# A second wide group in a feed-forward layer, transposes from raw copies, and three weight sums made earlier, in a two-layer hybrid trunk

## The chip, the cores and the metric

The kernel runs on one core of a Trainium2 chip. The metric is the device time of one execution in microseconds (us). Before the change the median of three runs is 2246.27 us (2244.93 to 2246.49).

## The reference, cut to what matters

Two layers over a sequence of 256 tokens of width 2048, batch 1, all in fp32. The mixers (a state-space scan beside block attention in layer 0, sparse attention beside retention in layer 1) are left out here; the change touches what stands around them.

```python
def layer_norm(x, g, b):
    mu = x.mean(-1, keepdims=True); var = jnp.square(x - mu).mean(-1, keepdims=True)
    return (x - mu) * lax.rsqrt(var + 1e-5) * g + b
# each layer, ALPHA = 4 ** 0.25:
#   x = layer_norm(ALPHA * x + mixer(x))
#   x = layer_norm(ALPHA * x + ffn(x))
# ffn: a and u are x @ w_up (2048 -> 5632 each), a depthwise causal convolution of 3 taps along the
#   tokens and a SiLU on a, then (a * u) @ w_down (5632 -> 2048)
```

## The kernel before, in words

**Numbers and products.** An fp32 value is split into a high part in fp32r (a 32-bit type that TensorE multiplies in one pass) and a low rest, and a product is the sum of high x high, high x low and low x high. Activations stand transposed in tiles `x` and `g`: 128 channels (a "k-tile") on the partitions, and along the free axis 256 tokens of high parts and 256 of low parts. Weights come as slabs of 128x1024 (two k-tiles of 512 columns, 512 KB): SP's queue loads `wraw`, ScalarE makes `whi` (L211), VectorE makes `wlo` (L219).

**Groups.** A projection is a row of groups, and PE runs them one behind the other. `group_b` (L432) makes 256 output channels from 16 k-tiles, in two halves of 128: for each k-tile and half a matmul of 512 columns with `whi` and one of 256 with `wlo`, so 64 matmuls for 2048 input channels. `group_m` (L544 to L546, "wide") makes the 1024 channels of four such groups, and takes two k-tiles (a pair) at a time with seven block products in place of eight (Strassen's way). It needs sums of weight blocks. A pair of k-tiles is plain ("P"), or its sums are made while it runs, by four VectorE adds in `add_up` (L230, "N"), or it reads sums that were made earlier and stored ("R", a "kept set"). A kept set is made by `Weights.make`: POOL's queue loads 1 MB of weights into `sums` (L241), VectorE adds (L251), POOL's queue stores the sums to `sumdown` (L255). `cycles` spaces these three steps over a list.

**The feed-forward layer** (`ffn`) has 44 groups of the up projection, for channel block j an a-group and a u-group. Where j is in `WIDE_UP`, one `group_m` of 180 matmuls takes the place of four groups (a and u of j and of j+1). Before, layer 0 has one (j = 7) and layer 1 has three (4, 8, 12). Such a result comes out with tokens on the partitions. It is put together in the tile `other` by VectorE adds (L562) and must be transposed on TensorE by sixteen 128x128 transposes in four bursts (`turn`, L1712). In layer 1 these are fp32 transposes straight from `other` with the matrix `ident`. In layer 0 each quarter of `other` is first copied by a DMA of POOL's queue into the fp32r tile `turned` (L1665), and the transposes run in fp32r with `unit`, a copy of the identity in that type. The tiles of a wide group (`other`, `turned`, `room`) lie in a pool that is given back after group `FIRST`.

**The norms.** The mixers and the first feed-forward layer leave their output in `r` (tokens on the partitions). There are three norms inside the trunk (idx 0, 1, 2) and one at its end. Their first k-tiles are normalized ahead (`norm`); `norm_full` does the others in pairs, while the first group of the next projection runs: four transposes of `r` (L847, fp32 with `ident`), then ScalarE and VectorE scale and split into `x`. When it has transposed k-tiles 4 and 5, it subtracts the mean and scales on VectorE for k-tiles 8 to 11 (`centre`, L798, one instruction for each token half), and with k-tiles 8 and 9 the same for 12 to 15. The group of L432 that runs meanwhile needs k-tile after k-tile of `x`.

**Order.** Steps that belong beside a projection lie in two lists, `self.fill` and `self.aux`; one step of each is taken between k-tiles. A scheduler then sets the order of each engine; instructions under `pin` keep the order of the program among themselves.

Of the kernel before, what the change touches and what calls it, by code (L numbers as in the profile page):

```python
# [9 lines left out]
F32 = mybir.dt.float32  # L10
F32R = mybir.dt.float32r
# [24 lines left out]
WIDE_UP = ((7,), (4, 8, 12))  # L36
FIRST = (22, 30)
# [16 lines left out]
EARLY = 2  # L54
# [272 lines left out]
class Trunk:  # L327
# [194 lines left out]
    def group_m(self, act, src, p, c, gap=1, fresh=None, inner=None):  # L522
# [26 lines left out]
        def fold():  # L549
# [3 lines left out]
            if fresh is not None or inner:  # L553
# [16 lines left out]
                for q, z in zip((0, 2, 1, 3), ((0, 0, "P2", e, OP.add), (1, 0, "P4", h, OP.subtract),  # L570
                                               (0, 1, "P3", g, OP.add), (1, 1, "B8", i, OP.add))):
                    fill.add(lambda z=z, q=q: (last(*z), self.copy and inner and self.copy(q)))
                if inner:
                    inner([[e, g], [h, i]])
# [265 lines left out]
    def norm_full(self, idx, k0):  # L840
# [4 lines left out]
        for i, k in enumerate(ks):  # L845
            for t in range(2):
                nc.tensor.transpose(ps[:, 256 * i + 128 * t:256 * i + 128 * t + 128], r[:, t, 128 * k:128 * k + 128],  # L847
                                    self.ident)
# [317 lines left out]
    def even(self):  # L1166
        nc, x = self.nc, self.x
        with ExitStack() as ctx:
# [63 lines left out]
            with self.tc.tile_pool(name="even2", bufs=1) as P2:  # L1232
# [8 lines left out]

                for i in range(4):
# [10 lines left out]
                    self.pair(heads, (2, 1, 1) if i < 2 else (0, 1, 1))  # L1253
                self.fill.rate = 1.0
# [153 lines left out]
    def odd(self):  # L1408
        nc, x = self.nc, self.x
        with ExitStack() as ctx:  # L1410
            P = ctx.enter_context(self.tc.tile_pool(name="odd", bufs=1))
            self.zbufs = 4
            y = P.tile([128, KT, 512], F32R, name="y")
            with self.tc.tile_pool(name="odd2", bufs=1) as P2:
# [85 lines left out]
                early = self.keys("down1")[:EARLY]  # L1500
                self.cycles(early, [slots], 14, self.aux)
# [134 lines left out]
    def ffn(self, layer):  # L1636
        nc, x = self.nc, self.x
        with ExitStack() as ctx:
# [9 lines left out]
            keys = self.keys("down0", "od_out") if layer == 0 else self.keys("down1")[EARLY:]  # L1648
            left = [double]
            if wide:  # L1650
                E = early.enter_context(self.tc.tile_pool(name="early", bufs=1))
                other = self.w.other = E.tile([128, 2048], F32, name="other")
                room = E.tile([128, 1024], F32, name="room")
# [7 lines left out]
            self.copy = None  # L1661
            if layer == 0:
                turned, unit = E.tile([128, 4, 512], F32R, name="turned"), E.tile([128, 128], F32R, name="unit")
                nc.scalar.activation(unit, self.ident, AF.Copy)
                self.copy = lambda q: self.pin(nc.gpsimd.dma_start(turned[:, q, :].bitcast(F32),  # L1665
                                                                   other[:, 512 * q:512 * q + 512]))
# [38 lines left out]
            def inner(j0):  # L1705
                def turn(j, own, evac):
# [176 lines left out]
```

## Time and profile before

| what | number |
|---|---|
| median of three runs | 2246.27 us (2244.93 to 2246.49) |
| the profiled execution's own time | 2247.41 us |
| its span in the profile | 2245.6 us |
| granted TensorE clock, mean | 0.999 |
| layer 0's feed-forward up projection and what follows up to the next mixer | about 378 to 861 us |
| layer 1's | from about 1527 us |

Rows that begin with an engine are one instruction, or a run of alike ones: start in us, length in us, engine, line of the kernel, operation, output<-inputs (buffer numbers left out), tile sizes, count, and in brackets how long the engine was idle ahead of it and what ended that. "128*128" is the weight block of a matmul. A matmul's length reaches over its pipeline, so two in a row overlap and the pitch between starts is the cost. Rows of windows give for each engine its busy time and its count of instructions in a stretch, the granted clock ("PEclk", 1.00 is full), the share of DMA time and GB/s. In a row of DMA issues the last number is the median time in us from the issue to the landing of the data.

### The profile page before, as it was taken

To read this page: it belongs to the slowest core of one execution; us is meant where nothing else is said; L and a number is where in the kernel's file an instruction comes from. 1 tells how busy PE (TensorE), PEld (TensorE's weight loads), DVE (VectorE), ACT (ScalarE), POOL (GpSimd) and SP (SyncE) were. 2 spreads that over 40 slices of the span, in tenths; PEclk is the share of its full clock that TensorE was granted. 3 is DMA by queue.
4 is the path that set the end of the run, shared out by engine and by line. 5 is a ranking of instruction groups with operands and counts; after the bars stand their busy time and mean duration, and the time that the engine had idled before them with its cause. 6 is when DMAs were issued, how large, how long until landed. Compare 5 with 4: busy or idle time off the path is not lost.

```text
span 2245.6 us, 32854 instructions
## 1 busy us (share of the span) xinstructions
PE 2236.6 (100%) x12061; PEld 1920.2 (86%) x12061; DVE 1829.0 (81%) x2772; ACT 1253.6 (56%) x1719; POOL 128.9 (6%) x223
## 2 busy tenths in 40 slices
PE   9999999999999999999999999999999999999998
PEld 9888888888888888888898888888888888888887
DVE  5788688988877778887977877889998887779887
ACT  5555556655655556656545564457555565557563
POOL 0101000110111110000000000000100001100000
PEclk9999999999999999999999999999999999999999
DMA  8855456796888886888667644567866768878784
GB/s 312 292 174 161 158 195 185 274 376 215 276 307 307 306 301 217 293 282 278 208 216 275 225 157 154 147 209 235 274 224 215 245 215 273 300 268 275 274 283 167
DMA packets 159098, 547.36 MB, mean 244 GB/s; under 512 B 17891, under 2 KB 19347, under 8 KB 158803
## 3 DMA queue, kind: packets, MB, share of 16 engines
q1 hardware_dynamic: 132937, 451.41, 60.4%
q0 software_dynamic: 25856, 93.60, 11.7%
q8 instruction: 94, 1.54, 0.3%
q14 instruction: 67, 0.55, 0.1%
q10 hardware_dynamic: 144, 0.26, 0.0%
HBM read 502.19 MB, written 41.96 MB: 242 GB/s over the span
## 4 chain that ended last, share of the span: by engine, by line
PE 96%; DVE 2%; issue 1%; DMA 1%; ACT 0%; POOL 0%; SPq 0%; ACTq 0%; DVEq 0%; POOLq 0%
PE acc L432 51%; PE ps L545 7%; PE ps L544 7%; PE ps L546 7%; PE acc L632 3%; PE acc L545 3%; PE acc L633 3%; PE acc L546 3%; PE acc L634 3%; PE acc L544 3%; PE ps L634 1%; PE ps L633 1%; PE ps L632 1%; PE ps L1160 1%; PE ps L432 1%
## 5 line engine op out<-in xcount | busy, mean ns | idle before, releaser
L211 ACT ACTIVATE whi<-wraw 128x1024 fp32r<-128x1024 f32 (+4 forms) x882 | 875.0, 1002 | 544.6 <-PE acc L432 215.1
L219 DVE TENSOR_TENSOR wlo<-wraw,whi 128x1024 fp32r<-128x1024 f32 (+4 forms) x882 | 1006.7, 1152 | 201.1 <-ACT whi L211 189.5
L432 PE MATMUL acc<-x,whi 128*128 128x512 f32 x3296 | 1033.1, 399 | 0.0
L432 PEld LDWEIGHTS acc<-x,wlo 128*128 128x128 f32 x3296 | 604.5, 188 | 135.8 <-DVE wlo L219 0.3
L432 PE MATMUL acc<-x,wlo 128*128 128x256 f32 x3296 | 634.4, 279 | 0.0
L432 PEld LDWEIGHTS acc<-x,whi 128*128 128x128 f32 x3296 | 511.0, 189 | 10.1 <-issue 0.9
L694 ACT ACTIVATE tmp<-acc 128x512 f32<-128x512 f32 x104 | 62.2, 598 | 169.2 <-PE acc L432 169.1
L251 DVE TENSOR_TENSOR sums<-sums 128x512 f32<-128x512 f32 (+1 forms) x112 | 87.5, 781 | 21.1 <-DMA sums<-in_down 19.5
L544 PE MATMUL ps<-whi,g 128*128 128x512 f32 x260 | 101.3, 390 | 0.1
L545 PE MATMUL ps<-wlo,g 128*128 128x512 f32 x260 | 101.4, 390 | 0.0
L546 PE MATMUL ps<-whi,g 128*128 128x512 f32 x260 | 101.3, 390 | 0.0
L545 PE MATMUL ps<-wlo,x 128*128 128x512 f32 x244 | 95.7, 392 | 0.1
L546 PE MATMUL ps<-whi,x 128*128 128x512 f32 x244 | 95.1, 390 | 0.0
L544 PE MATMUL ps<-whi,x 128*128 128x512 f32 x244 | 94.5, 390 | 0.0
L632 PE MATMUL acc<-whi,x 128*128 128x344 f32 (+3 forms) x224 | 75.3, 339 | 0.1
L633 PE MATMUL acc<-wlo,x 128*128 128x344 f32 (+3 forms) x224 | 74.7, 333 | 0.0
L1690 DVE SCALAR_TENSOR_TENSOR c<-fpad,prm,c 128x256 f32<-128x256 f32 x176 | 74.0, 479 | 0.8 <-ACT c L1687 0.7
L634 PE MATMUL acc<-whi,x 128*128 128x344 f32 (+3 forms) x224 | 74.4, 332 | 0.0
L211 ACT ACTIVATE whi<-other 128x1024 fp32r<-128x1024 f32 x32 | 33.7, 1054 | 54.9 <-DVE other L230 54.5
L255 POOL DMA_DIRECT2D sumdown<-sums x58 | 31.2, 537 | 527.0 <-DVE sums L251 526.7
L544 PEld LDWEIGHTS ps<-whi,g 128*128 128x128 f32 x260 | 48.8, 188 | 10.7 <-DVE r L712 0.5
L545 PEld LDWEIGHTS ps<-wlo,g 128*128 128x128 f32 x260 | 48.8, 188 | 10.5 <-DVE wlo L219 0.4
(465 smaller groups left out, 3144.5 us busy)
## 6 DMA issues: line engine op xcount, KB each, us to landing
wraw<-in_up SPq DMA_DIRECT2D x328, 512.0 KB, 4.8
wraw<-in_down SPq DMA_DIRECT2D x142, 512.0 KB, 4.9
wraw<-in_od_in SPq DMA_DIRECT2D x96, 512.0 KB, 4.1
wraw<-in_ev_in SPq DMA_DIRECT2D x72, 512.0 KB, 4.1
wraw<-sumdown SPq DMA_DIRECT2D x68, 512.0 KB, 4.9
sums<-in_down POOLq DMA_DIRECT2D x58, 512.0 KB, 7.1
sumdown<-sums POOLq DMA_DIRECT2D x58, 512.0 KB, 4.9
wraw<-in_ev_out SPq DMA_DIRECT2D x30, 512.0 KB, 3.9
```

What stands on the lines that cost most here:

```text
L211: a = nc.scalar.activation(hi[:, :n], raw[:, :n], AF.Copy)
L219: b = nc.vector.tensor_tensor(lo[:, :n], raw[:, :n], hi[:, :n].bitcast(F32), op=OP.subtract)
L251: self.tc.keep_in_program_order(nc.vector.tensor_tensor(o, x, y, op=OP.add))
L432: nc.tensor.matmul(acc, wt, mv, start=(k == 0 and i < len(unit)), stop=(k == nk - 1 and i >= len(unit)))
L544: nc.tensor.matmul(o, xh, wh, start=n not in used, stop=False)
L545: nc.tensor.matmul(o, xh, wl, start=False, stop=False)
L546: nc.tensor.matmul(o, xl, wh, start=False, stop=stop)
L632: nc.tensor.matmul(o, xh, wh, start=start, stop=False)
L633: nc.tensor.matmul(o, xh, wl, start=False, stop=False)
L634: nc.tensor.matmul(o, xl, wh, start=False, stop=stop)
L694: nc.scalar.activation(t, a[:, :, 256:], AF.Copy, scale=sign)
L1690: nc.vector.scalar_tensor_tensor(c[:, i, :], pad[:, i, t:t + 256], w[:, t:t + 1], c[:, i, :], op0=OP.mult, op1=OP.add)
```

## The change

- Layer 0's wide groups are 4 and 8 in place of 7, and `FIRST` for layer 0 is 24 in place of 22.
- In layer 1 the wide groups 4 and 8 (not 12, the last) are turned from raw copies too: after the group's last L562, one DMA of 128x4x256 (512 KB, POOL's queue) brings the columns of block j, a second one those of j+1, and the transposes run in fp32r with `unit`. `turned` takes the room of `room`, which is given back when the first wide group starts.
- In the norms 0, 1 and 2, right after each `centre` of k-tiles 8 to 11 and 12 to 15 a DMA on POOL's queue copies the centred 128x512 (256 KB) of `r` into a tile that is free at that time (`part` in the feed-forward layers, `y` in the odd mixer), and `norm_full` transposes these eight k-tiles from the copies, in fp32r.
- `unit` is made once, behind the first mixer, in the tile of `ones`.
- Three kept sets of layer 0's down projection are made during layer 0's attention (list `aux`, one each 14 steps), no longer in its feed-forward layer. Layer 1's two early sets stay.

```diff
-WIDE_UP = ((7,), (4, 8, 12))
-FIRST = (22, 30)
+WIDE_UP = ((4, 8), (4, 8, 12))
+FIRST = (24, 30)
-EARLY = 2
+EARLY = (3, 2)
 # norm_full
-                nc.tensor.transpose(ps[:, 256 * i + 128 * t:256 * i + 128 * t + 128], r[:, t, 128 * k:128 * k + 128],
-                                    self.ident)
+                to, src, by = ps, r[:, t, 128 * k:128 * k + 128], self.ident
+                if k >= 8:
+                    c = 512 * t + 128 * (k % 4)
+                    to, src, by = ps.bitcast(F32R), self.copies[k // 4 - 2][:, c:c + 128], self.unit
+                nc.tensor.transpose(to[:, 256 * i + 128 * t:256 * i + 128 * t + 128], src, by)
...
         if k0 % 4 == 0 and k0 + 4 < KT:
             for t in range(2):
-                self.pin(self.centre(t, 128 * k0 + 512, 512))
+                c = 128 * k0 + 512
+                self.pin(self.centre(t, c, 512))
+                self.pin(nc.gpsimd.dma_start(self.copies[k0 // 4 - 1][:, 512 * t:512 * t + 512].bitcast(F32),
+                                             r[:, t, c:c + 512]))
 # even, ahead of the attention's heads
+                self.aux.add(12)
+                self.cycles(self.keys("down0")[:EARLY[0]], [self.w.sums], 14, self.aux)
 # ffn
-            keys = self.keys("down0", "od_out") if layer == 0 else self.keys("down1")[EARLY:]
+            keys = self.keys(*(("down0", "od_out"), ("down1",))[layer])[EARLY[layer]:]
+                self.copies = self.slots[:1:-1]
 # ffn, inner
+                width = 0 if layer and j0 == wide[-1] else turned.shape[2]
+                def copy(q, c):
+                    src = blocks[:, q, :] if width == 512 else blocks[:, :, c:c + width]
+                    to = turned[:, q, :] if width == 512 else turned
+                    self.pin(nc.gpsimd.dma_start(to.bitcast(F32), src))
...
+                    for i, j in enumerate((j0, j0 + 1)):
+                        if width == 256:
+                            aux.add(lambda i=i: copy(0, 256 * i), 3)
 # warm_up and run
+        self.unit = self.consts.tile([128, 128], F32R, name="ones")
+        nc.scalar.activation(self.unit, self.ident, AF.Copy)
```

How the order of PE moves at the norm ahead of layer 0's feed-forward layer (idx 0), k-tiles 6 and 7 of its first group, with the transposes of k-tiles 8 and 9 among them. Before:

```order
L432 MATMUL acc<-x,whi 128x512 x4
L432 MATMUL ps<-x,whi 128x512 x2
L847 MATMUL ps<-ident,r 128x128 x2
L432 MATMUL acc<-x,wlo 128x256 x4
L432 MATMUL ps<-x,wlo 128x256 x2
L847 MATMUL ps<-ident,r 128x128 x2
L432 MATMUL acc<-x,whi 128x512 x2
L432 MATMUL acc<-x,wlo 128x256 x2
```

After (`part_3662` is the raw copy of k-tiles 8 to 11):

```order
L432 MATMUL acc<-x,whi 128x512 x4
L432 MATMUL ps<-x,whi 128x512 x2
L432 MATMUL acc<-x,wlo 128x256 x4
L432 MATMUL ps<-x,wlo 128x256 x2
L851 MATMUL ps<-ones,part_3662 128x128
L432 MATMUL acc<-x,whi 128x512 x2
L851 MATMUL ps<-ones,part_3662 128x128 x3
L432 MATMUL acc<-x,wlo 128x256 x2
```

Of the four transposes, the first of token half 0 now stands behind six `wlo` matmuls, and the three others two 512-column matmuls later; whatever comes behind them on PE waits until the copies have landed.

How POOL moves in the same place, from the end of layer 0's scan to the start of its feed-forward layer. Before:

```order
L1367 TENSOR_TENSOR xs<-xs 128x256 x3
L1377 TENSOR_TENSOR rms<-rms,mhalf 128x2
L1367 TENSOR_TENSOR xs<-xs 128x256 x3
L1377 TENSOR_TENSOR rms<-rms,mhalf 128x2
L794 TENSOR_TENSOR rs<-mv,mhalf 128x1 x2
L874 DMA room<-in_lnrow 128x512 x2
L241 DMA sums<-in_down 128x1024 x2
L241 DMA second<-in_down 128x1024 x2
```

After, the end of the same stretch (`sumdown_5` is the third of the kept sets that are now made in the attention):

```order
L241 DMA sums<-in_down 128x1024 x2
L255 DMA sumdown_5_0_1764<-sums 128x1024
L255 DMA sumdown_5_1_1765<-sums 128x1024
L794 TENSOR_TENSOR rs<-mv,mhalf 128x1 x2
L866 DMA part_3662<-r 128x512 x2
L866 DMA part_3661<-r 128x512 x2
L880 DMA room<-in_lnrow 128x512 x2
L241 DMA sums<-in_down 128x1024 x2
L241 DMA second<-in_down 128x1024 x2
```

The loads and stores of three kept sets stand ahead of the norm, and the four copies of the norm stand ahead of the loads of the residual's rows (`room`) and of the next kept sets.

More of the change, by code (lines that the diff above doesn't have):

```diff
@@ L571, in fold @@
                                                (0, 1, "P3", g, OP.add), (1, 1, "B8", i, OP.add))):
-                    fill.add(lambda z=z, q=q: (last(*z), self.copy and inner and self.copy(q)))
-                if inner:
-                    inner([[e, g], [h, i]])
+                    fill.add(lambda z=z: last(*z))
+                    if inner:
+                        inner(q)
                 return
@@ L1660, in ffn @@
                 self.residual(2 * layer, [[self.spare[:, 0:512], self.spare[:, 512:1024]]] * 4)
[L1661 to L1666, printed above, removed]
             if double:
@@ L1705, in inner @@
             def inner(j0):
-                def turn(j, own, evac):
+                turned, aux = turning[0], self.aux
+                width = 0 if layer and j0 == wide[-1] else turned.shape[2]
+                sides = turned if width else other.rearrange("p (q c) -> p q c", q=4)
+                blocks = other.rearrange("p (q c) -> p q c", q=4)
+                def copy(q, c):
+                    src = blocks[:, q, :] if width == 512 else blocks[:, :, c:c + width]
+                    to = turned[:, q, :] if width == 512 else turned
+                    self.pin(nc.gpsimd.dma_start(to.bitcast(F32), src))
@@ L1707, in turn @@
+                def turn(j, n, evac):
                     ps = self.ps()
-                    to, unit_ = (ps.bitcast(F32R), unit) if self.copy else (ps, self.ident)
+                    to, by = (ps.bitcast(F32R), self.unit) if width else (ps, self.ident)
                     for o in range(2):
                         for t in range(2):
-                            c = 256 * (j - j0) + 128 * o
-                            nc.tensor.transpose(to[:, 256 * o + 128 * t:256 * o + 128 * t + 128], own[t][:, c:c + 128], unit_)
+                            c = (256 * (j - j0) + 128 * o) % (width or 512)
+                            nc.tensor.transpose(to[:, 256 * o + 128 * t:256 * o + 128 * t + 128],
+                                                sides[:, 2 * t + n, c:c + 128], by)
@@ L1713, in turn, with go @@
                     evac(ps.rearrange("p (a b) -> p a b", a=2), False)
-                def go(z):
-                    if self.copy:
-                        z = [[turned[:, 2 * t + n, :] for n in range(2)] for t in range(2)]
-                        self.aux.add(3)
-                    for j in (j0, j0 + 1):
+                def go(q):
+                    if width == 512:
+                        aux.q.append(lambda last=aux.q.pop(): (last(), copy(q, 0)))
+                    if q < 3:
+                        return
+                    for i, j in enumerate((j0, j0 + 1)):
+                        if width == 256:
+                            aux.add(lambda i=i: copy(0, 256 * i), 3)
+                        elif width and i == 0:
+                            aux.add(2)
@@ L1720, in go @@
                         for n, f in enumerate((ev_a, ev_u)):
-                            self.aux.add(1, lambda j=j, n=n, f=f: turn(j, [z[t][n] for t in range(2)], f(j)))
+                            aux.add(1, lambda j=j, n=n, f=f: turn(j, n, f(j)))
                 return go
@@ L1735, in ffn @@
                     assert not self.aux.q
+                    if j == wide[0]:
+                        rooms.close()
+                        turning.append(rooms.enter_context(self.tc.tile_pool(name="turned", bufs=1)).tile(
+                            [128, 4, 256 if layer else 512], F32R, name="turned"))
                     self.group_m(x, f"up{layer}", wide.index(j), 0, inner=inner(j))
```

13 lines of the change are left out of this document (8 added, 5 removed).

## The prediction

> **What bounds the kernel now.** I read the page's busy times first, then its chain of waits. The first says which engine has no slack, the second whether that engine also sets the end.
>
> ```profile
> PE 2236.6 (100%) x12061; PEld 1920.2 (86%) x12061; DVE 1829.0 (81%) x2772; ACT 1253.6 (56%) x1719; POOL 128.9 (6%) x223
> ```
>
> The chain, as shares by engine:
>
> ```profile
> PE 96%; DVE 2%; issue 1%; DMA 1%; ACT 0%; POOL 0%; SPq 0%; ACTq 0%; DVEq 0%; POOLq 0%
> ```
>
> PE is busy throughout and carries 96% of the chain, so what PE no longer executes comes off the time, and every wait put into PE's order is added in full. An added copy or sum costs something only where PE comes to wait for it. Windows then give the price of the groups, and how full VectorE (DVE) is where the change loads it.
>
> ```profile
> core 0: us, PE busy (x) PEld busy (x) DVE busy (x) ACT busy (x) POOL busy (x), PEclk, DMA share, GB/s
> 528.38:569.66 41.28, 41.27 (x181) 33.64 (x180) 36.76 (x43) 24.11 (x27) 0.56 (x1) 1.00 0.64 198
> 569.66:861.40 291.74, 291.74 (x1682) 255.10 (x1681) 217.85 (x264) 154.28 (x190) 31.84 (x59) 1.00 0.84 294
> 1610.19:1652.28 42.09, 41.65 (x181) 33.55 (x180) 38.41 (x46) 24.21 (x27) 0.00 (x0) 1.00 0.66 218
> 180.00:276.00 96.00, 96.00 (x607) 84.03 (x606) 68.67 (x134) 50.87 (x89) 8.19 (x7) 1.00 0.50 160
> 378.00:423.00 45.00, 45.00 (x266) 39.42 (x266) 44.60 (x84) 35.01 (x57) 2.13 (x4) 1.00 0.80 272
> 1250.00:1340.00 90.00, 90.00 (x540) 79.83 (x539) 67.29 (x199) 53.44 (x141) 3.75 (x7) 1.00 0.56 188
> ```
>
> The rows are, in this order: layer 0's wide group; the stretch behind it, up to the end of its feed-forward up projection; layer 1's first wide group; layer 0's attention; the start of layer 0's feed-forward layer; layer 1's second half of the mixer. The granted clock is 1.00 everywhere, so it does not enter.
>
> **Cheaper transposes.** A burst of four in fp32r, then one in fp32, each with what stands behind it:
>
> ```profile
> 582.22 0.46 PE L1712 MATMUL ps<-unit,turned 128*128 128x128 f32 x4
> 582.51 0.70 PE L432 MATMUL acc<-x,whi 128*128 128x512 f32 x2
> 583.05 0.28 PE L432 MATMUL acc<-x,wlo 128*128 128x256 f32 x1
> ```
>
> and
>
> ```profile
> 1660.63 0.60 PE L1712 MATMUL ps<-ident,other 128*128 128x128 f32 x4
> 1660.99 0.71 PE L432 MATMUL acc<-x,whi 128*128 128x512 f32 x2
> 1661.54 0.40 PE L432 MATMUL acc<-x,wlo 128*128 128x256 f32 x2
> ```
>
> From start to start: 0.29 + 0.54 = 0.83 against 0.36 + 0.55 = 0.91, so a burst saves 0.08. Two groups of layer 1 have 8 bursts (**-0.6**), three norms with k-tiles 8 to 15 have 12 (**-0.9**). The Trainium skill (FP8 and Floating Point Precision, TensorE Precision Notes) says that true fp32 takes four passes through the array. By that rule an fp32 burst would cost 4 x 0.29 = 1.2 and the 20 bursts would save some 17 us; the rows show 0.36, so the trace does not agree for transposes.
>
> **One more wide group.** The stretch of 291.74 us holds 26 groups of L432 (1664 of its 1682 matmuls), the four bursts of turns and nothing else of size on PE. By the rows above a burst of four fp32r turns costs about 0.37: 0.29, and 0.08 because the two matmuls behind it take 0.54 and not the usual 0.47 or so. So four groups cost (291.74 - 4 x 0.37) / 26 x 4 = 44.7. The wide group that replaces them costs 41.3 and its own four bursts 1.5: a gain of 1.9. Layer 0's first wide group now stands at j = 4, where layer 1's first one stands. That one took 42.1, and its PE waited for `wlo`:
>
> ```profile
> 1614.43 0.51 PE L545 MATMUL acc<-wlo,part 128*128 128x512 f32 x1 [0.44 <-DVE wlo L219]
> ```
>
> DVE's order is the same at that place, so I charge 0.8 for it. Net: **-1.1** (-1.9 without that charge).
>
> **Do the norms' copies come in time?** This is the large term. The rows that set it are those of idx 0: `centre` on DVE, PE at the burst for k-tiles 8 and 9 and at the one for 12 and 13, and, for the time that such a copy takes, layer 0's turns, which copy the same 256 KB from tile to tile on the same queue.
>
> ```profile
> 379.27 1.00 DVE L798 TENSOR_SCALAR r<-r,mv,rs 128x512 f32<-128x512 f32 x2
> 386.64 1.00 DVE L798 TENSOR_SCALAR r<-r,mv,rs 128x512 f32<-128x512 f32 x2
> 381.88 0.38 PE L847 MATMUL ps<-ident,r 128*128 128x128 f32 x2
> 382.19 0.74 PE L432 MATMUL acc<-x,wlo 128*128 128x256 f32 x4
> 383.00 0.38 PE L847 MATMUL ps<-ident,r 128*128 128x128 f32 x2
> 392.06 0.60 PE L847 MATMUL ps<-ident,r 128*128 128x128 f32 x4
> ```
>
> and the turns, with the landing of their copies in the last row:
>
> ```profile
> 574.64 0.68 DVE L562 TENSOR_TENSOR other<-ps,other 128x512 f32<-128x512 f32 x1
> 573.13 0.56 POOL L1665 DMA_DIRECT2D turned<-other  x1 [3.51 <-DVE other L562]
> 574.00 0.55 POOL L1665 DMA_DIRECT2D turned<-other  x1 [0.31 <-issue]
> 575.64 0.55 POOL L1665 DMA_DIRECT2D turned<-other  x1 [1.09 <-DVE other L562]
> L1665 POOL DMA_DIRECT2D turned<-other x4: 546/551/556, 569.1 to 575.6; - x4
> DMA to landing us min/median/max: 4.1/4.6/5.3
> ```
>
> A copy starts 0.3 us behind the DVE instruction that it reads (575.64 against 574.64 + 0.68), and a second one 0.87 behind the first (574.00 - 573.13). The first of the pair's two instructions ends half-way, at 379.8, so the copies start at 380.1 and 381.0, and the second lands at 381.0 + 4.6 = 385.6. By its new order PE is past the six `wlo` matmuls at 382.7 (383.00 less the 0.31 of the two transposes that left), then does one transpose of half 0 and two matmuls (0.5), and needs half 1 at 383.2. First wait: 385.6 - 383.2 = 2.4.
>
> The wait delays the next `centre`, which needs what this burst brings: 3.64 us lie between 383.00 and 386.64. Counted from the burst, its first half ends at 3.64 + 0.5, the copies start at 4.5 and 5.35, and the second lands at 9.95. PE's next burst came 392.06 - 383.00 = 9.06 behind, less the two matmuls that now stand ahead and the burst's own saving: 8.5. Second wait: 1.45. It may be a little shorter. What DVE does with the burst waits for ScalarE's copy of it and for four slabs of `wlo`:
>
> ```profile
> 383.88 0.56 ACT L855 ACTIVATE sums<-ps,prm 128x256 f32<-128x256 f32 x1
> 381.18 3.56 DVE L219 TENSOR_TENSOR wlo<-wraw,whi 128x768 fp32r<-128x768 f32 x4
> 384.65 0.42 DVE L858 TENSOR_TENSOR x<-sums,x 128x256 fp32r<-128x256 f32 x1
> ```
>
> ScalarE ended at 384.44, DVE began at 384.65. While PE stands DVE does these slabs, so I take off that 0.2 and have 1.2, and 3.6 for the norm.
>
> ```profile
> 1098.56 1.00 DVE L798 TENSOR_SCALAR r<-r,mv,rs 128x512 f32<-128x512 f32 x2
> 1528.11 1.00 DVE L798 TENSOR_SCALAR r<-r,mv,rs 128x512 f32<-128x512 f32 x2
> 1105.88 0.60 PE L847 MATMUL ps<-ident,r 128*128 128x128 f32 x4
> 1531.84 0.38 PE L847 MATMUL ps<-ident,r 128*128 128x128 f32 x2
> ```
>
> Idx 2 has the same spacing (1531.84 - 1528.11 = 3.73, as 383.00 - 379.27), so another 3.6. Idx 1 has 7.32 between `centre` and burst; its second copy starts at 1100.3 and lands by 1105.6 even with the 5.3 of the longest row (0.3 of room), so I charge no wait there. Sum: **+7.2**. The ends: with 4.1 for a copy 1.9 + 0.7 in each norm, +5.2; with 5.3 and nothing taken off 3.1 + 2.15, +10.5; and the nearest rows of another queue:
>
> ```profile
> wraw<-in_od_in SPq DMA_DIRECT2D x8, 256.0 KB, 2.7
> sums<-in_down POOLq DMA_DIRECT2D x58, 512.0 KB, 7.1
> ```
>
> With 2.7 the first wait is 0.5, the second nothing: +1.0. I take the row of POOL's queue, since the copies are on it. The Trainium skill (DMA: Bandwidth & Descriptors, Anatomy of one DMA, the SWDGE path) gives 2.0 us and the bytes over 436 KB per us. That is an estimate of 2.6 for 256 KB, and the norms would then cost +0.8; the 4.1 to 5.3 of this trace disagree with it.
>
> POOL's queue has these four copies ahead of the residual's rows and the next kept set, so those come up to 3.5 us later (4 x 0.87). They feed sums that are due tens of us later (layer 0's first wide group now starts some 60 us behind this), so nothing is charged; if that cover is gone, the late thing is a set's L251, ahead of `wlo` on DVE, and the price is that of the DVE rival.
>
> **Layer 1's turn copies.** The order puts the first turn of these groups behind 40 pairs of L432 matmuls where it stood behind 24: 16 x (0.23 + 0.12) = 5.6 us later than 1660.63, at 1666.2.
>
> ```profile
> 1657.26 0.68 DVE L562 TENSOR_TENSOR other<-ps,other 128x512 f32<-128x512 f32 x1
> ```
>
> The copy starts at 1657.94 + 0.3 and has 8.0 us; 512 KB on this queue take 7.1 in the median. So 0, with up to 1.5 a group if it is slow. The steps that come between take none of PE.
>
> **Kept sets in the attention.** The adds of all kept sets are one group of the page:
>
> ```profile
> L251 DVE TENSOR_TENSOR sums<-sums 128x512 f32<-128x512 f32 (+1 forms) x112 | 87.5, 781 | 21.1 <-DMA sums<-in_down 19.5
> ```
>
> There are 29 sets (58 loads of half a set each, x58 above), so a set costs DVE 87.5 / 29 = 3.0 us. Three make 9 on top of 68.67 in the 96 us of layer 0's attention. Layer 1's mixer carries two such sets in 90 us with DVE at 67.29, and PE is busy for all 90.00 of it. So 0, at most 1.5; what would be late is a `wlo`. What leaves the feed-forward layer gives nothing back, since PE did not wait there either. The one ScalarE copy that makes `unit` stands behind the mixer's end: 0.2 at most, 0 taken.
>
> **Sum.** -1.1 - 0.6 - 0.9 + 7.2 = +4.6. Against the profiled execution's own 2247.41 that is 2252.0; against the median, which lies 1.14 below it, 2250.9.
>
> **The rivals.** *The copies are hidden* (the other side: not slower). If 256 KB between tiles land in 2.7 us or less at these places, as SP's rows do, the norms cost 1.0 and the sum is -1.6: 2244.7. The deciding point is a landing of 2.2 (383.2 - 381.0) for no wait at all and of about 3.5 for a sum of zero (1.3 in each norm). For it: the copies are alone on POOL's queue at that time. Against it: all four rows of 4.1 to 5.3, taken at a DMA share of 0.84 as against 0.80 here. *Only the first wait of each norm is real*, since DVE catches up while PE stands: +4.8 in place of +7.2, 2248.5. I count it as the lower part of the forecast. *DVE becomes the bound in layer 0's feed-forward layer*: it is busy 44.60 of 45.00 us from 378 on, and two wide groups add their sums. If each of the eight pairs of the two groups whose sums are made on the fly lost the 0.8 of the first one, that would be 5.8 more than charged: 2256.7. Against it: layer 1's wide groups fit with DVE at 38.41 of 42.09. *Transposes in fp32 cost four times those in fp32r*: 0.8 more for each of 20 bursts, -16, about 2235. The two rows of this kernel exclude it nearly.
>
> **Chances.** The forecast has 0.60 (own range 2248.5 to 2254.2, by the ends of the norms' term and the case of one wait), the hidden copies 0.20, DVE 0.12, the dear transposes 0.02, and 0.06 is left for what I do not see. 0.2%, about the least that a measurement of this kernel tells from no change, is 4.5 us: 2241.8 to 2250.8. The forecast lies on the upper bound, so half of it, 0.30, is slower; with DVE and half of the rest that makes 0.45. Faster are the dear transposes and a little of the hidden copies, 0.05; the same 0.50. The range from 2243.2 to 2255.0 takes in the hidden copies and nearly all of the forecast.
>
> **What would show it.** In the changed kernel's trace PE should wait for a DMA of `part` at about 383 and 392 and at about 1532 and 1541, 2.4 and 1.2 us, not at 1106. The copies should land in 4.1 to 5.3. A wide group of layer 0 should take 41.3 to 42.1 and the bursts behind it 0.37. No PE wait should stand at layer 1's turns or in layer 0's attention. The prediction is wrong if the copies land within 2.7, or if the scheduler's place for them is not the one that PE reaches at 383.2 because DVE's `centre` comes earlier or later; and if a wait for `wlo` recurs in the wide groups.

## The result: slower by 14.5 us, and the profile after

The changed kernel takes 2260.57 us in the median of six runs (2258.07 to 2265.13) against 2246.07 for the kernel before in the same comparison (2244.93 to 2246.58). The ratio is 1.0069, with a 95% interval of 1.0058 to 1.0081. So it is slower, by about three times what was forecast, and above the range. Its runs also lie further apart: 7 us as against 2. The profiled execution is the fastest of the six (2258.07), so its trace shows the smallest of the losses. Two executions among the experiments below, of 7916 and 2754 us, lie far from all others of their kernels and are left out of the medians.

Busy times and the chain, from the page of the changed kernel:

```profile
PE 2235.2 (99%) x12001; PEld 1912.6 (85%) x12001; DVE 1846.1 (82%) x2800; ACT 1261.4 (56%) x1726; POOL 139.9 (6%) x243
```

```profile
PE 89%; issue 4%; DVE 3%; DMA 2%; POOL 0%; ACT 0%; SPq 0%; DVEq 0%; POOLq 0%; ACTq 0%
```

PE has 60 instructions and 1.4 us of work less than before, as the edits intend, and the span is 10.7 us longer. What PE waited for, from the view of waits (engine, line, what it waited for, us in total, times, longest):

```profile
PE ps L851 <- DMA part<-r: 3.4, 4, 1.2
PE acc L545 <- DVE wlo L219: 2.8, 3, 1.3
PE ps L1140 <- DVE z L1136: 2.4, 1, 2.4
PE ps L851 <- issue: 1.1, 1, 1.1
...
PE ps L1727 <- DMA turned<-other: 1.0, 1, 1.0
```

The first row was forecast. The fourth stands at the first burst of norm 2 that reads a copy (at 1538.45); the view names no releaser for it. The other three were forecast as nothing, or nearly. Windows by stage show where they lie. First the changed kernel: mixer of layer 0 with its attention; the first 464 matmuls of layer 0's feed-forward layer; its two wide groups; the first 464 matmuls in layer 1; the group ahead of layer 1's third wide group; that wide group.

```profile
52.98:279.74 226.76, 224.11 (x1363) 195.34 (x1362) 176.87 (x311) 121.42 (x182) 22.80 (x30) 1.00 0.68 226
381.77:467.70 85.93, 83.54 (x483) 72.12 (x482) 79.36 (x131) 53.63 (x79) 11.91 (x22) 1.00 0.86 291
467.70:511.59 43.89, 42.26 (x181) 33.39 (x180) 40.21 (x48) 24.31 (x27) 0.54 (x1) 1.00 0.61 196
557.71:598.95 41.24, 41.22 (x181) 33.59 (x180) 37.23 (x44) 24.11 (x27) 0.55 (x1) 1.00 0.66 211
1532.57:1618.34 85.77, 83.28 (x482) 72.17 (x481) 80.85 (x135) 53.66 (x79) 10.87 (x20) 1.00 0.82 276
1748.30:1795.59 47.29, 46.33 (x273) 40.49 (x272) 37.57 (x55) 27.00 (x36) 4.23 (x7) 1.00 0.70 239
1795.59:1838.82 43.23, 41.90 (x182) 33.45 (x180) 39.57 (x47) 24.22 (x27) 1.62 (x3) 1.00 0.75 253
```

The same stages in the kernel before, as far as it has them (layer 0's mixer, the first 464 matmuls in layer 1, the group ahead of the third wide group, and that group):

```profile
53.10:276.38 223.28, 223.28 (x1362) 195.58 (x1361) 170.78 (x302) 121.08 (x181) 16.53 (x18) 1.00 0.62 201
1527.25:1610.19 82.94, 82.94 (x483) 72.53 (x481) 80.84 (x136) 53.55 (x79) 8.63 (x16) 1.00 0.84 276
1739.98:1786.41 46.43, 46.43 (x273) 40.77 (x272) 40.74 (x58) 26.66 (x36) 2.81 (x6) 1.00 0.71 235
1786.41:1827.72 41.31, 41.30 (x181) 33.64 (x180) 36.78 (x43) 24.10 (x27) 1.46 (x3) 1.00 0.77 247
```

In each of these stages before, PE's busy time equals the stage, to 0.01. In the changed kernel it falls short by 2.65 in layer 0's mixer, 2.4 and 2.5 at the two norms, 1.6 in layer 0's first wide group, 1.0 ahead of layer 1's third and 1.3 in it. Norm 1 has no such wait: its stretch (1072.06 to 1141.67 in the changed kernel) is 0.3 shorter than before. The second wide group of layer 0 runs without a wait, in 41.24.

### The profile page after: what moved, and what is told of

The parts are those of the page before. It is cut to its first block, busy times and chain, and to the rows that moved or that the text cites. A ratio compares the mean times of both kernels' runs of the same rounds, so it can differ in the third digit from the quotient of the medians.

```text
span 2256.3 us, 32832 instructions
## 1 busy us (share of the span) xinstructions
PE 2235.2 (99%) x12001; PEld 1912.6 (85%) x12001; DVE 1846.1 (82%) x2800; ACT 1261.4 (56%) x1726; POOL 139.9 (6%) x243
## 4 chain that ended last, share of the span: by engine, by line
PE 89%; issue 4%; DVE 3%; DMA 2%; POOL 0%; ACT 0%; SPq 0%; DVEq 0%; POOLq 0%; ACTq 0%
PE acc L432 44%; PE ps L545 7%; PE ps L546 7%; PE ps L544 7%; PE acc L632 3%; PE acc L633 3%; PE acc L634 3%; PE acc L545 3%; PE acc L546 3%; PE acc L544 3%; DVE wlo L219 1%; PE ps L633 1%; PE ps L632 1%; PE ps L634 1%; DMA room<-in_lnrow 1%
## 5 line engine op out<-in xcount | busy, mean ns | idle before, releaser
L432 PE MATMUL acc<-x,whi 128*128 128x512 f32 x3168 | 993.7, 398 | 0.0
L432 PEld LDWEIGHTS acc<-x,wlo 128*128 128x128 f32 x3168 | 580.2, 188 | 131.7 <-DVE wlo L219 1.1
L432 PE MATMUL acc<-x,wlo 128*128 128x256 f32 x3168 | 609.4, 279 | 0.3 <-DVE wlo L219 0.2
L432 PEld LDWEIGHTS acc<-x,whi 128*128 128x128 f32 x3168 | 490.8, 189 | 9.8 <-issue 1.3
L545 PE MATMUL ps<-wlo,x 128*128 128x512 f32 x284 | 111.7, 393 | 0.8 <-DVE wlo L219 0.7
L546 PE MATMUL ps<-whi,x 128*128 128x512 f32 x284 | 110.6, 390 | 0.0
L544 PE MATMUL ps<-whi,x 128*128 128x512 f32 x284 | 109.9, 390 | 0.0
L211 ACT ACTIVATE whi<-other 128x1024 fp32r<-128x1024 f32 x40 | 42.1, 1053 | 73.7 <-DVE other L230 67.5
L545 PEld LDWEIGHTS ps<-wlo,x 128*128 128x128 f32 x284 | 53.3, 188 | 16.0 <-DVE wlo L219 4.9
L219 DVE TENSOR_TENSOR wlo<-other,whi 128x1024 fp32r<-128x1024 f32 x40 | 48.9, 1221 | 18.5 <-ACT whi L211 18.4
L544 PEld LDWEIGHTS ps<-whi,x 128*128 128x128 f32 x284 | 53.3, 188 | 11.5 <-issue 0.2
```

The source lines that it names most:

```text
L211: a = nc.scalar.activation(hi[:, :n], raw[:, :n], AF.Copy)
L219: b = nc.vector.tensor_tensor(lo[:, :n], raw[:, :n], hi[:, :n].bitcast(F32), op=OP.subtract)
L432: nc.tensor.matmul(acc, wt, mv, start=(k == 0 and i < len(unit)), stop=(k == nk - 1 and i >= len(unit)))
L544: nc.tensor.matmul(o, xh, wh, start=n not in used, stop=False)
L545: nc.tensor.matmul(o, xh, wl, start=False, stop=False)
L546: nc.tensor.matmul(o, xl, wh, start=False, stop=stop)
```

## The experiments

All were timed in five or more rounds against the kernel before, whose median in them was 2245.1 to 2245.5. It was 2246.07 beside the changed kernel, so a difference between a run here and the changed kernel carries up to 0.9 us of that drift, besides the spread of the runs.

**Undo one part at a time.** The kept sets first:

```diff
-EARLY = (3, 2)
+EARLY = (0, 2)
 # even
-                self.aux.add(12)
-                self.cycles(self.keys("down0")[:EARLY[0]], [self.w.sums], 14, self.aux)
```

> The changed kernel, but the three kept sets of layer 0's down projection are made in the feed-forward layer again, none in layer 0's attention. Theory A (in the attention DVE stands in L251, waiting for the load of a set, and the attention's softmax waits behind it): the 2.4 us wait of PE for z and the 3.5 us of that stretch go, the rest stays, so about 3.5 below the changed kernel (2260.6), 2257. Theory B (DVE simply has too much to do, wherever the sets stand): the same time comes back in the feed-forward layer, at the first wide group of layer 0 (43.9 in the changed kernel), and the total stays within 1 of 2260.6.

2265.61 (ratio 1.0087, 1.0072 to 1.0103): 5.0 slower than the changed kernel, which neither theory had. The attention's wait is gone, but another one came, which both had overlooked, at the start of layer 0's down projection (its view of waits, and the window over that stage, which takes 102.36 in the changed kernel):

```profile
PE ps L851 <- DMA part<-r: 5.8, 5, 1.9
...
PE ps L544 <- ACT x L342: 2.9, 2, 1.7
```

```profile
866.32:974.34 108.02, 104.73 (x451) 85.28 (x450) 96.20 (x149) 66.95 (x85) 4.29 (x8) 0.98 0.88 308
```

Of the 5.7 us that this stage is longer, PE stood for 3.3; the clock of 0.98 in the row is the subject of a paragraph further down. `L342` there writes the sums of `g` that the down projection multiplies (into the room of `x`). In the code these steps come in the list behind the feed-forward layer's kept sets. With a second wide group that layer has fewer steps for the list, so the move and the second wide group probably belong together; the sets put back with one wide group were not run. The waits at the norms, too, were longer in this run (5.8 against 3.4).

**The norms without copies.**

```diff
-                if k >= 8:
+                if k >= 8 and False:
...
-                self.pin(nc.gpsimd.dma_start(self.copies[k0 // 4 - 1][...].bitcast(F32), r[:, t, c:c + 512]))
```

> The changed kernel without the raw copies of the norms: k-tiles 8 to 15 are transposed in fp32 from r as before. Theory A (the copies land too late at norms 0 and 2): the stretches of 464 matmuls at the start of the two feed-forward layers shrink by about 3 each, the norm of idx 1 gains 0.3 less, total about 6 below the changed kernel, 2254.6. Theory B (the waits at the norms only use up slack that DVE needs anyway in the wide groups): the waits for wlo at the first wide groups grow and the total falls by less than 3. Theory C (the late copies also delay the sums for the first wide groups): these wide groups get faster too, by 1 to 2 each, and the total falls by 8 or more.

2254.55 (1.0041, 1.0028 to 1.0054), 6.0 below the changed kernel, as theory A had it. Both stretches are back at the length of before, with no wait:

```profile
382.81:465.78 82.97, 82.97 (x482) 72.49 (x481) 78.89 (x131) 53.45 (x79) 8.60 (x16) 1.00 0.84 283
1531.44:1614.38 82.94, 82.94 (x483) 72.47 (x481) 81.43 (x137) 53.67 (x79) 7.55 (x14) 1.00 0.80 271
```

The first wide group of layer 0 takes 44.3, where it took 43.9 in the changed kernel, so its waits do not come from the norm (against theory C). The five runs spread over 2.7 us as against 7. That the spread is the copies' alone is not shown: with the copies in place and the sets spaced (below) it is 3.3.

**One wide group in layer 0**, as before:

```diff
-WIDE_UP = ((4, 8), (4, 8, 12))
-FIRST = (24, 30)
+WIDE_UP = ((7,), (4, 8, 12))
+FIRST = (22, 30)
```

> The changed kernel with one wide group in layer 0 (7, FIRST 22) as before. Theory A (the first wide group at j = 4 waits 2.6 for VectorE, and the second one gains 1.9): both nearly cancel, total within 1.5 of the changed kernel, 2260.6. Theory B (the second wide group is a clear gain even so): 1 to 2 slower than the changed kernel. Theory C (the place j = 4 is what makes DVE late, later stretches included): 2 or more faster.

2257.97 (1.0052, 1.0039 to 1.0066), 2.6 below the changed kernel: by the number it is theory C, but both kernels spread by 4 us or more, and the stages behind layer 0 keep their times (the third wide group of layer 1 takes 43.65), which speaks against it. It is taken to say that in this surrounding the second wide group brings no gain. The last experiments measure it without the norms' spread.

**Layer 1's turns in fp32 from `other`**, as before:

```diff
-                width = 0 if layer and j0 == wide[-1] else turned.shape[2]
+                width = 0 if layer else turned.shape[2]
```

> The changed kernel with layer 1's wide groups turned in fp32 straight from the tile other, as before. Theory A (the copies of the second group land late by 1.1, and the turns, now later, put VectorE work next to the third wide group, which costs 1.9): both waits go and the fp32 transposes cost 0.6, about 2.4 below the changed kernel, 2258. Theory B (the waits there are due to the shift of everything ahead): within 1 of 2260.6.

2256.91 (1.0052, 1.0040 to 1.0065), 3.7 below the changed kernel. The third wide group takes 41.3 again, the group ahead of it 46.4. Theory A, with a larger price than it had; from layer 1's first wide group to its third the profile has 2.9 less.

**Same work, at another time.** The sets of the attention spaced differently:

```diff
-                self.aux.add(12)
-                self.cycles(self.keys("down0")[:EARLY[0]], [self.w.sums], 14, self.aux)
+                self.aux.add(2)
+                self.cycles(self.keys("down0")[:EARLY[0]], [self.w.sums], 18, self.aux)
```

> The changed kernel with the three sets of layer 0's attention spaced 18 steps apart and begun 10 steps earlier, so that 9 steps instead of 5 lie between the loads of a set and its adds; the number of instructions is the same. Theory A (DVE stands in front of L251 until the load has landed, 3.5 us in the changed kernel, and z waits behind it): that idle time goes, the stretch from 53 us falls from 226.8 to about 223.5, total about 3 below the changed kernel (2260.6), 2257.5. Theory B (the 9 us of adds themselves are too much for DVE in this stretch): the stretch stays within 1 of 226.8 and the total within 1.

2255.69 (1.0045, 1.0033 to 1.0058), 4.9 below the changed kernel. The mixer's stretch:

```profile
53.21:276.76 223.55, 223.53 (x1363) 195.38 (x1361) 177.75 (x311) 121.39 (x182) 23.20 (x30) 1.00 0.69 229
```

DVE does as much as in the changed kernel there (177.75 against 176.87), and PE does not wait. So it is theory A: the order, not the amount. The stretch is 3.2 shorter, as theory A had it. The 4.9 is not its price alone: in this run layer 0's first wide group took 42.6 in place of 43.9, and layer 1's third one 41.3 in place of 43.2. The rows of the changed kernel, POOL, DVE and PE in turn:

```profile
222.21 1.41 POOL L1376 TENSOR_TENSOR xs<-xs 128x256 f32<-128x256 f32 x1 [8.38 <-ACT xs L1373]
224.50 0.74 POOL L1376 TENSOR_TENSOR xs<-xs 128x256 f32<-128x256 f32 x1 [0.88 <-ACT xs L1373]
225.18 1.11 POOL L241 DMA_DIRECT2D sums<-in_down  x2
```

```profile
228.35 1.23 DVE L219 TENSOR_TENSOR wlo<-wraw,whi 128x1024 fp32r<-128x1024 f32 x1 [1.10 <-ACT whi L211]
233.12 1.23 DVE L251 TENSOR_TENSOR sums<-sums 128x1024 f32<-128x1024 f32 x1 [3.54 <-DMA sums<-in_down]
```

```profile
245.25 0.30 PE L1140 MATMUL ps<-ident,z 128*128 128x128 f32 x1 [2.39 <-DVE z L1136]
```

The second set's loads stand on POOL behind `xs`, which waits for ScalarE, and so start at 225.2. DVE reaches the adds at 229.6, stands for 3.5, then works without a gap until 245.7 with `z` and `wlo` behind the adds, and PE has to wait for `z`. With the wider spacing the loads were out at 201.6 and the adds at 222.8 found them landed.

**The norms' copies, a step earlier:**

```diff
 # norm, at its end (t == 1)
+            self.copied(1024)
 # norm_full
-        if k0 % 4 == 0 and k0 + 4 < KT:
-            for t in range(2):
-                ...
+        if k0 == 4:
+            self.copied(1536)
+    def copied(self, c):
+        for t in range(2):
+            self.pin(self.centre(t, c, 512))
+            self.pin(self.nc.gpsimd.dma_start(self.copies[c // 512 - 2][...].bitcast(F32), self.r[:, t, c:c + 512]))
```

> The changed kernel with the norms' centre and copy of k-tiles 8 to 11 issued already with the head of the norm, and those of 12 to 15 where those of 8 to 11 were, so each copy has one step of four k-tiles more; the amount of work is the same. Theory A (the copies only land too late, by 1 to 3 us): PE's waits for part go in both feed-forward layers, the stretches of 464 matmuls fall from 85.8 to 89.6 to at most 82.9, total 6 to 7 below 2260.6, 2254, and the spread over the runs shrinks. Theory B (a copy of this size on this queue takes as long as the DMA engines' other traffic makes it, and gets in the way of the weights): waits for whi or wlo take the place of those for part, total within 3 of 2260.6. Theory C (DVE is so full at the norm's head that 1 us more of centre there costs the same on PE): total 2 to 4 below only.

2254.94 (1.0039, 1.0026 to 1.0053), 5.6 below, within a few tenths of leaving the copies out, and the spread shrank to 3 us. But the stretches took 84.3 and 84.4, not 82.9: PE's wait for `part` fell to 1.4, and a wait for `x`, 0.8 in two pieces, came with the earlier `centre` (theory C for that part).

```profile
PE ps L852 <- DMA part<-r: 1.4, 2, 0.8
...
PE acc L432 <- DVE x L862: 0.8, 2, 0.4
```

**Turns in fp32, at the later places:**

```diff
-                width = 0 if layer and j0 == wide[-1] else turned.shape[2]
+                width = 0 if layer else turned.shape[2]
...
+                        elif not width and j0 != wide[-1]:
+                            aux.add(4)
```

> The changed kernel with layer 1's wide groups turned in fp32 straight from the tile other, but at the places of the changed kernel (behind 40, 48, 72 and 80 pairs of matmuls of the next groups, not 24 to 48). Theory A (the later turns bring their VectorE work next to the third wide group, whose PE then waits for wlo): the third wide group keeps its 43.2 as against 41.3, the group ahead loses its wait for turned (47.3 to about 46.5), total about 1 below 2260.6. Theory B (the third group's wait follows from the late copy): both go, as in the run with the turns at their old places, 2257.

2256.46 (1.0051, 1.0038 to 1.0063), 4.1 below the changed kernel; the third wide group takes 41.28:

```profile
1799.07:1840.35 41.28, 41.23 (x182) 33.60 (x181) 36.78 (x43) 24.10 (x27) 1.08 (x3) 1.00 0.75 239
```

So theory A is wrong and B right: the third group's wait belongs to the copies, not to the place of the turns. How, the changed kernel's rows suggest (POOL, then DVE, then PE, and the DMA engines' share from 1770 to 1780):

```profile
1768.78 0.54 POOL L255 DMA_DIRECT2D sumdown<-sums  x1 [1.46 <-DVE c L1695]
1769.42 0.77 POOL L1719 DMA_DIRECT2D turned<-other  x1
1771.03 0.54 POOL L241 DMA_DIRECT2D sums<-in_down  x1 [0.85 <-DMA sumdown<-sums]
```

```profile
1779.39 0.69 DVE L230 TENSOR_TENSOR other<-wraw 128x512 f32<-128x512 f32 x1 [4.44 <-DMA wraw<-in_up]
```

```profile
1775.27 0.53 PE L1727 MATMUL ps<-ones,turned 128*128 128x128 f32 x4 [0.96 <-DMA turned<-other]
1801.01 0.50 PE L545 MATMUL acc<-wlo,part 128*128 128x512 f32 x1 [1.30 <-DVE wlo L219]
```

```profile
1770.00:1780.00 10.00, 9.04 (x55) 7.82 (x55) 4.47 (x7) 6.51 (x9) 1.25 (x3) 1.00 0.97 359
```

The second copy stands on POOL behind the stores of a kept set, starts at 1769.4, and lands 5.8 later, 1.0 too late for PE. The stores, the copy, the next set's loads and the weights share DMA engines that are 97% busy. DVE stands 4.4 before an add of weight sums, and is then without a gap until PE needs `wlo` in the wide group. Before, the same DVE instruction stood 1.98. That DVE's standing causes the wide group's wait is the likely link, not a shown one: with spaced sets DVE stood 3.9 there and the group took 41.3, after PE had already lost 1.7 at the turn and some 1.5 behind it (at a lower clock, see below).

**Layer 0's wide groups one block later:**

```diff
-WIDE_UP = ((4, 8), (4, 8, 12))
+WIDE_UP = ((5, 9), (4, 8, 12))
```

> The changed kernel with layer 0's wide groups at 5 and 9 in place of 4 and 8: the first one starts about 22 us later, with the same work. Theory A (at j = 4 DVE has not yet caught up with the norm's and the residual's work): the first wide group falls from 43.9 to 41.3 to 42, total 2 to 2.5 below 2260.6. Theory B (DVE's load is that of the wide group itself with the kept sets beside it, wherever it starts): it stays at 43 to 44 and the total within 1.

2258.32 (1.0063, 1.0050 to 1.0075), 2.3 below. The first wide group took 42.55 where the others had 42.6 to 44.3 at j = 4. It points to A at most: the spaced sets had 42.56 at j = 4, and the difference of the totals is within the scatter of the runs.

**The norms' copies alone**, put into the kernel before:

```diff
 # norm_full; `copies` and `unit` as in the change, nothing else of it
-                    self.ident)
+                if k >= 8:
+                    to, src, by = ps.bitcast(F32R), self.copies[k // 4 - 2][:, c:c + 128], self.unit
...
+                self.pin(nc.gpsimd.dma_start(self.copies[k0 // 4 - 1][...].bitcast(F32), r[:, t, c:c + 512]))
```

> The kernel before with the norms' raw copies alone (k-tiles 8 to 15 of norms 0, 1, 2 transposed from copies), nothing else changed. Theory A (each of the norms 0 and 2 makes PE wait for its copies, whatever else the kernel does): the stretches of 464 matmuls grow by 3 to 5 each as in the changed kernel, norm 1 gains 0.3, total 5 to 8 above the kernel before (2245.2), about 2251. Theory B (the copies are late only because the other edits load the DMA queues): 0 to 2 above before.

2252.77 (1.0032, 1.0020 to 1.0044), 7.2 above before; the runs spread from 2250.25 to 2256.09. Theory A: the price of the copies does not need the rest of the change.

**What comes behind a wait: a stretch at half the clock.** The prediction left the clock out, and in the changed kernel's own trace it is 1.00 from the first microseconds to the last ones. In other executions it is not. The second wait of norm 0, first in the changed kernel, then in the run with layer 1's turns in fp32, whose code at this place is the same: the end of the wait, the next burst, and 3.4 us between them.

```profile
398.59 0.45 PE L851 MATMUL ps<-ones,part 128*128 128x128 f32 x3 [1.19 <-DMA part<-r]
403.13 0.46 PE L851 MATMUL ps<-ones,part 128*128 128x128 f32 x4
399.95:403.35 3.40, 3.40 (x24) 3.00 (x22) 3.08 (x9) 1.66 (x4) 0.00 (x0) 1.00 0.76 271
```

```profile
399.24 0.44 PE L851 MATMUL ps<-ones,part 128*128 128x128 f32 x3 [1.29 <-DMA part<-r]
405.34 0.46 PE L851 MATMUL ps<-ones,part 128*128 128x128 f32 x4
400.60:404.00 3.40, 3.40 (x13) 2.91 (x12) 2.39 (x6) 1.44 (x3) 0.00 (x0) 0.50 0.70 261
```

In the second execution the granted clock is 0.50 for 3.4 us, PE gets through 13 matmuls where it did 24, and the next burst comes after 6.1 in place of 4.5: 1.6 us that no view of waits shows. The eight traces that have the norms' copies at the places of the change show it behind the second wait of norm 0 in six, behind that of norm 2 in three, behind the wait for `z` in two (once at each of these two places for 6.8 us), behind the turn with the spaced sets, and in the down projection of the first experiment, where the clock of 0.98 is this. It begins between 0.7 us ahead of the end of the wait and 1.6 us behind it. The kernel before, and the three kernels without the copies below, show it only at the end of the program. The mean clock of whole executions fits: 0.997 to 0.999 in the six of the changed kernel, 0.999 or 1.000 in all of the kernel before beside the experiments. It is not the whole spread (one execution of the changed kernel has 0.999 and took 2264.19), and what decides whether a wait is followed by such a stretch stays open: the trace of the changed kernel has the same waits and none.

**What is left without the copies.** Norms in fp32 and layer 1's turns in fp32, sets spaced by 18, with two wide groups at 4 and 8, at 5 and 9, and with one at 7:

```diff
 # in all three, the edits shown above
+                if k >= 8 and False:
+                width = 0 if layer else turned.shape[2]
+                self.aux.add(2)
+                self.cycles(self.keys("down0")[:EARLY[0]], [self.w.sums], 18, self.aux)
 # and one of these
 WIDE_UP = ((4, 8), (4, 8, 12))
+WIDE_UP = ((5, 9), (4, 8, 12))
+WIDE_UP = ((7,), (4, 8, 12))   # FIRST = (22, 30)
```

> The changed kernel with the norms in fp32 from r, layer 1's turns in fp32 at their old places, and the sets of the attention spaced 18 steps: of the change there remain the second wide group in layer 0 and the three sets made in the attention. Theory A (the three waits found are the whole loss): 2245 to 2246.5, since the second wide group's gain of 1.9 is eaten in part by the wait for wlo of the first one (42.5 to 43.9 as against 41.3). Theory B (something else is slower too): 2248 or more.

> As the run with two wide groups and none of the copies, with the groups at 5 and 9 in place of 4 and 8. Theory A (the later place leaves DVE time to catch up): the first wide group takes 41.3 to 42.5, total about 1 below that run, 2244.5, which would be below the kernel before. Theory B (the place makes no difference without the norms' waits): within 0.5 of it.

> As the run with two wide groups and none of the copies, with one wide group (7) as before; so it is the kernel before with three sets moved into the attention, 18 steps apart. Theory A (spaced like this, moving the sets costs nothing and gives nothing): within 1 of before (2245.2). Theory B (the feed-forward layer gains by having fewer sets): 1 to 2 below. The difference to the run with two groups is the second group's own gain: 1.9 if nothing waits, near 0 if the first group waits as it did.

| layer 0's wide groups | median, us | ratio to before | interval | first wide group |
|---|---|---|---|---|
| 4 and 8 | 2247.18 | 1.0005 | 0.9996 to 1.0014 | 43.15 |
| 5 and 9 | 2244.57 | 0.9996 | 0.9987 to 1.0004 | 41.84 |
| 7 alone | 2246.27 | 1.0004 | 0.9995 to 1.0013 | 41.24 |

None differs from before by more than its interval. Between each other, eleven runs each, the order is clear enough to read with the rows: at 4 and 8 the first group waits and the second one's gain is eaten (0.9 slower than one group); at 5 and 9 it is 1.7 faster than one group, near the 1.9 worked out for it. In the profiles the up projection with the groups at 5 and 9 takes 481.6 and the one with a single group 483.0, so 1.4 less, with 0.6 still lost in the first group. Windows over the first wide group at j = 4, and at j = 5, from those two kernels:

```profile
461.78:504.93 43.15, 41.94 (x181) 33.46 (x180) 39.52 (x47) 24.33 (x27) 0.54 (x1) 1.00 0.63 197
```

```profile
484.05:525.89 41.84, 41.61 (x181) 33.52 (x180) 38.16 (x45) 24.37 (x28) 0.54 (x1) 1.00 0.66 213
```

The later group has 1.4 us less of DVE work beside it, and PE waits 0.2 instead of 1.2. That is 1.3 of the 2.6 between the two medians. In the trace with 4 and 8, layer 1's first wide group lost 1.9 too, though the code there is the same as in the others; that group takes 41.3 to 43.9 over all traces. This is the best version found, with 1.0 below before in the median; its interval still reaches over 1.

## Why the prediction was wrong, point by point

- **The norms' copies: the wait is right, its size in part by luck.** Forecast +7.2 for the waits, -0.9 for cheaper transposes, so +6.3. Measured: 6.0 by leaving them out, 7.2 by putting them in alone. But PE stood only 4.4 to 6.3 at these bursts over the eight traces, and the stretches at half clock, which the prediction did not have ("every wait put into PE's order is added in full"), make up for that in most of them. Norm 1 is hidden, as forecast. The two waits of a norm were forecast as 2.4 and 1.2. At norm 0 they are 0.4 and 1.9 in the changed kernel's trace, at norm 2 1.1 and 1.1, and in the seven other traces the second is always the longer one. The landing is not one number:

```profile
387.67 0.45 PE L851 MATMUL ps<-ones,part 128*128 128x128 f32 x3 [0.36 <-DMA part<-r]
397.15 0.25 PE L851 MATMUL ps<-ones,part 128*128 128x128 f32 x1 [0.69 <-DMA part<-r]
398.59 0.45 PE L851 MATMUL ps<-ones,part 128*128 128x128 f32 x3 [1.19 <-DMA part<-r]
```

The first pair of copies landed 2.6 and 3.2 after its issue (and PE came to it 0.7 later behind `centre` than forecast), the second one, with the residual's rows loaded right behind it, 4.5 and 5.5. The prediction compared the DMA share of the turns and of the norm as 0.84 and 0.80, but these are means over 292 and 45 us. In the kernel before, where the turns' copies were under way it is 0.96, at the norm's first burst 0.66 and at its second 0.90 (windows 573 to 581, 380 to 388 and 388 to 395):

```profile
573.00:581.00 8.00, 8.00 (x48) 7.03 (x47) 4.71 (x5) 2.59 (x3) 2.73 (x5) 1.00 0.96 335
380.00:388.00 8.00, 8.00 (x49) 6.92 (x49) 8.00 (x15) 5.74 (x9) 0.00 (x0) 1.00 0.66 205
388.00:395.00 7.00, 7.00 (x43) 6.16 (x42) 6.87 (x15) 5.45 (x11) 0.00 (x0) 1.00 0.90 297
```

- **The kept sets in the attention: the step that failed first.** Forecast 0, at most 1.5; the stretch lost 3.5 against before, of which spacing alone takes back 3.2 (4.9 in the medians, with other waits that went at the same time). The prediction compared DVE's busy time with the window (68.67 + 9 of 96) and called it room. The loss came from order: an add that waits for its load holds up all of DVE, and the load itself stood on POOL behind work that waited for ScalarE. It had looked at layer 1's two sets, which have no such neighbour on POOL.
- **Layer 1's turn copies: failed.** Forecast 0, up to 1.5 a group; measured 3.7 in the medians and 2.9 in the profiles. The 8 us of room were counted for the first copy of a group. The second one starts when the queue ahead of it lets it, behind a kept set's stores, and the price has a second part, the third wide group's wait for `wlo`, which the prediction did not have. Of the gain, the cheaper bursts are there: the group behind the first wide group of layer 1 takes 46.1 in place of 46.4, as forecast (4 x 0.08).
- **The second wide group: gain right, cover wrong.** It takes 41.24 as forecast and its own gain, where next to nothing waits, is 1.7 (1.9 forecast). At j = 4 it is lost, since the first wide group costs 42.6 to 44.3 over the runs and not 42.1. The 42.1 was one draw: that group of layer 1 takes 41.3 to 43.9 over all traces. So -1.1 was forecast and +0.9 came. The rival that DVE becomes the bound named this place; its price, 0.8 for each of eight pairs (5.6 more than charged, not the 5.8 that stands there), is not what happened: in the changed kernel four waits of 0.2 to 0.6 in the first group, none in the second.
- **Sum.** In the profiled execution, stage by stage against before: norms +5.5, layer 0's mixer +3.5, layer 1's three wide groups and the groups between them +3.0, layer 0's up projection behind its norm +0.7, all else -1.9 (1.3 of it in layer 1's mixer); together, to rounding, the 10.7 of the span. The forecast had only the first term and 1.7 of gains. In the medians the edits give 6.0 for the norms, 4.9 for the sets and 3.7 for the turns. These must not be added up, though they happen to make the 14.5: spacing the sets and undoing the turns both took the wait of layer 1's third wide group. With all three edits the kernel comes to 2247.18, 1.6 above before and within its interval, so together they hold nearly the whole loss. Why most executions lost more than the profiled one is explained by the clock only in part.

## What to carry to other kernels

Where PE is always busy, an operation "beside" it is free only if nothing stands behind its wait: look for each moved load, add or copy at what is queued ahead of it on its own queue and what is queued behind the instruction that waits for it, not at the busy share. The same three sets cost 3.2 us of their stage at one spacing and no wait at another. A share of DMA time says something about a copy's landing only over the microseconds of that copy, not as a mean over a stage. And a wait of 1 to 3 us can cost more than itself: here a stretch at half clock followed it in some executions and not in others, so one trace is not enough to price it. A copy through a DMA queue to save 0.08 us of a transposition pays only if its landing, at its slowest, is far from the time of need.

## What the runs showed of the hardware that was not expected

The time that a 256 KB copy between tiles on POOL's queue takes to land went with the share of DMA time in the same few microseconds (the copies themselves are part of it):

| place | window, us | DMA share | landings, us |
|---|---|---|---|
| norm 0, first pair | 383.80 to 388.00 | 0.68 | 2.6, 3.2 |
| norm 2, first pair | 1534.00 to 1539.00 | 0.71 | 3.2, 3.2 |
| norm 1, first pair | 1106.40 to 1110.90 | 0.77 | 2.3, 3.3 |
| norm 1, second pair | 1118.30 to 1122.90 | 0.89 | 3.1, 4.0 |
| norm 2, second pair | 1543.00 to 1549.00 | 0.91 | 3.8, 4.8 |
| norm 0, second pair | 392.50 to 399.00 | 0.94 | 4.5, 5.5 |
| layer 0's turns, before | 573.00 to 581.00 | 0.96 | 4.1 to 5.3 |

So the landing of before, 4.1 to 5.3, is one of a busy stretch. No run changed the load alone, so that the load sets the landing is the likely reading, not a shown one. The Trainium skill's fit (DMA: Bandwidth & Descriptors, Anatomy of one DMA, the SWDGE path) gives an estimate of 2.6 us for such a copy. The landings of 2.3 to 3.3 at shares up to 0.77 agree with that, those of 3.1 to 5.5 at shares from 0.89 do not. The changed kernel's windows at the two pairs of norm 0:

```profile
383.80:388.00 4.20, 3.69 (x21) 2.49 (x20) 4.20 (x7) 2.36 (x4) 1.15 (x2) 1.00 0.68 222
392.50:399.00 6.50, 4.62 (x29) 3.82 (x28) 5.60 (x11) 3.53 (x7) 2.14 (x4) 1.00 0.94 300
```

The other unexpected fact is the clock: 0.50 for 3.4 us (twice 6.8) around or behind the end of a wait of PE, in some executions and not in others, at some 1.5 us for each 3.4.
